# Attention: a head's gate steps and transposes spread over the next head, and the second map's factor as two tensor_tensor steps

## The chip, the cores and the metric

The kernel runs on one NeuronCore of a Trainium2 chip. The metric is the device time of one execution in microseconds (us). TensorE (PE in the profile) multiplies and transposes, VectorE (DVE) and ScalarE (ACT) do elementwise work, GpSimd (POOL) too, and SyncE (SP) issues the DMAs.

## What is computed

One streaming step of a layer with two token mixers: a gated linear recurrence and a differential attention, projected, merged and added to the input. There are 2048 prompt tokens and 64 sample tokens with 4096 cached keys, 8 heads with two maps of 64 channels each, and values of 128 channels. The change lies in the attention and its output norm and gate:

```python
def diff_attn(q, k, v, q_pos, k_pos, rel_bias, lam):
    s = jnp.einsum('bqhmd,bkhmd->bhmqk', q, k) * (DK ** -0.5)
    s = jnp.where(visible, s + bias, -jnp.inf)
    p = jax.nn.softmax(s, axis=-1)
    w = p[:, :, 0] - lam * p[:, :, 1]
    return jnp.einsum('bhqk,bkhd->bqhd', w, v)

o = rms_norm(o, subln_gain) * (1.0 - lam_init)
yb = o.reshape(B, T, W_B) * jax.nn.silu(zb)
```

## The kernel before

The program goes through a first stage (norm of the input, recurrence), projections, the attention stage (1659 to 2551 us of the profile), and output projections. Within attention the 8 heads follow each other. A head has 16 query blocks of 128 tokens, taken in 8 pairs in the order `ORDER`, large beside small, and a block of sample queries (`sample_score_units`, `sample_turn_units`) between them.

A query block's scores come, for each of the two maps, in units of up to 1024 columns: `product` (L942, L943) writes them into a bank `pk` (two buffers), `evacuate` empties it on VectorE with the bias added and the maximum taken (L955, L963) into `S0`/`S1` or, for short blocks, `T0`/`T1`. L972 makes the maximum `nm`; ScalarE takes the exponential with its sum (L973). Behind the second map, VectorE computes the factor `cf` = -lambda · sum0 / sum1, one element a partition: a reciprocal (L978) and a step with two products (L979). GpSimd multiplies the second map by `cf` (L980) and adds it to the first (L981). Then TensorE transposes the result in groups of up to four (L1000), ScalarE copies it (L1001), and TensorE multiplies it with the values (L1008). The sample's scores come in four steps of 1024 cached keys (L1063) and one of 64 new ones (L1077); VectorE evicts the first two into `SA` and the next two into `SB` (L1067, the last in two pieces, L1072), and the fifth by L1078.

When a head's last value product is done, `finish` runs in the time of the next head: it computes the norm's factor with small steps (L1155 to L1160 and three rounds of `newton`, L55 to L57), and then for five chunks of up to four query blocks `weigh` loads the gate `zt` (three buffers) and does one `scalar_tensor_tensor` (L1172) for each block, 17 for a head; `part` transposes them (L1182) into `ptt` (three buffers), evicts that with a gain into `yt` (L1184, two buffers) and stores it in `yb_d` (L1185).

TensorE's order in this stage is written by a planner: a loop with a model time `pe[0]` takes score, transpose and value units as they come due. `extras` holds work with a due time; its entries run as soon as `pe[0]` has reached it. `finish` is such an entry, `part` of chunk j another, due 12 + 1.5·j model-us later (3 + 1.5·j in the last head); `weigh` runs in `finish` itself, for all five chunks. The order on VectorE, ScalarE, GpSimd and SyncE is chosen by the scheduler from this program.

Of the kernel before, what the change touches and what calls it, by code (L numbers as in the profile page):

```python
# [14 lines left out]
ALU = mybir.AluOpType  # L15
# [10 lines left out]
NH = 8  # L26
# [301 lines left out]
def stream_step_kernel(ctx, tc, I, O):  # L328
    nc = tc.nc
# [27 lines left out]
    neglam = cst.tile([P, 1], F32, name="neglam")  # L357
# [505 lines left out]
    with ExitStack() as c:  # L863
# [57 lines left out]
        def score_units(h, hd, Q, i, st):  # L921
# [23 lines left out]
            def evacuate(m, u):  # L945
# [8 lines left out]
                if f > 0:  # L954
                    nc.vector.tensor_scalar(  # L955
                        s[:, k0 : k0 + f], pk[:, :f], far[:, h : h + 1], None,
                        op0=ALU.add, op1=ALU.max, accum_out=mp[:, cx["j"] : cx["j"] + 1],
                    )
                    cx["j"] += 1
                if f < w:  # L960
# [4 lines left out]
                        op0=ALU.add, op1=ALU.max, accum_out=mp[:, cx["j"] : cx["j"] + 1],  # L965
# [4 lines left out]
                sc = [st[f"s{r}"][:, i : i + 1] for r in range(2)]  # L970
# [5 lines left out]
                S = cx["S"]  # L976
                cf = wk.tile([P, 1], F32, name="cf", bufs=4)
                nc.vector.reciprocal(cf, sc[1])  # L978
                nc.vector.scalar_tensor_tensor(cf, cf, sc[0], neglam, op0=ALU.mult, op1=ALU.mult)  # L979
                nc.gpsimd.tensor_scalar(S[1][:, :n], S[1][:, :n], cf, 1.0, op0=ALU.mult, op1=ALU.mult)  # L980
                nc.gpsimd.tensor_tensor(S[0][:, :n], S[0][:, :n], S[1][:, :n], op=ALU.add)  # L981

# [168 lines left out]
        def finish(h, t0, n, st):  # L1151
# [12 lines left out]
            def weigh(b, nb):  # L1164
                tn = TOK[b][1]
                zt = wk.tile([P, 4, P], F32, name="zt", bufs=3)
                nc.sync.dma_start(
                    zt[:tn, :nb, :], zb_d[b : b + nb, :tn, h * P : (h + 1) * P].rearrange("b p c -> p b c")
                )
                for j in range(nb):  # L1170
                    k = b + j
                    nc.vector.scalar_tensor_tensor(  # L1172
                        o[:tn, k, :], o[:tn, k, :], y[:tn, k - t0 : k - t0 + 1], zt[:tn, j, :],
                        op0=ALU.mult, op1=ALU.mult,
                    )
                book("dve", pe[0] + 2.0, 0.25 * nb)
# [10 lines left out]
            for j, b in enumerate(range(t0, t0 + n, 4)):  # L1187
                nb = min(4, t0 + n - b) if b < NT - 1 else 1
                if b < NT - 1 < b + nb:
                    nb = NT - 1 - b  # L1190
                weigh(b, nb)
                extras.append([pe[0] + (12.0 if h < NH - 1 else 3.0) + 1.5 * j, 0.11 * nb,
                               lambda b=b, nb=nb: part(b, nb)])


# [1 line left out]
        pe = [0.0]  # L1197
# [25 lines left out]
        extras = []  # L1223
# [329 lines left out]
```

## Time and profile before

| | |
|---|---|
| time, median of 3 (lowest, highest) | 3129.71 us (3129.59, 3131.15) |
| the profiled execution: time, span | 3132.76 us, 3131.0 us |
| mean granted clock of TensorE | 0.958 |
| busy in the whole span: PE, DVE, ACT, POOL | 91%, 66%, 54%, 46% |
| L979, 128 times | 65.1 us of DVE |
| L1172, 128x128, 128 times | 48.4 us of DVE |
| L1184, 128x512, 31 times | 23.1 us of DVE |

A row of the timeline is one instruction, or several of one kind in a row ("x12", with the length of all). In brackets stands the idle time of the engine before it, and what ended that. An instruction that is held while it executes is shown longer, not as idle. In the table by stretch, the granted clock stands as a share of 2.4 GHz; the lower level, 1.2 GHz, is 0.5.

### The profile page before, as it was taken

To read this page: it belongs to the slowest core of one execution; us is meant where nothing else is said; L and a number is where in the kernel's file an instruction comes from. 1 tells how busy PE (TensorE), PEld (TensorE's weight loads), DVE (VectorE), ACT (ScalarE), POOL (GpSimd) and SP (SyncE) were. 2 spreads that over 40 slices of the span, in tenths; PEclk is the share of its full clock that TensorE was granted. 3 is DMA by queue.
4 is the path that set the end of the run, shared out by engine and by line. 5 is a ranking of instruction groups with operands and counts; after the bars stand their busy time and mean duration, and the time that the engine had idled before them with its cause. 6 is when DMAs were issued, how large, how long until landed. Compare 5 with 4: busy or idle time off the path is not lost.

```text
span 3131.0 us, 43652 instructions
## 1 busy us (share of the span) xinstructions
PE 2854.5 (91%) x14808; PEld 2392.7 (76%) x14808; DVE 2070.2 (66%) x4147; ACT 1703.7 (54%) x3251; POOL 1447.7 (46%) x900
## 2 busy tenths in 40 slices
PE   6999996999979989699997998998999979979899
PEld 6888885777758777587785987887888768868677
DVE  7776786267685776735525677777777775475764
ACT  7776774345544455545445766676676653333432
POOL 0000005355454544545544655555465457786743
PEclk9999998999989999899998999999999989989999
DMA  4121232335534346354346453544543434545553
GB/s 139 60 75 53 70 122 84 124 128 149 181 100 156 129 131 184 108 165 138 107 117 170 124 141 112 144 127 122 135 117 116 128 101 148 196 149 196 177 172 129
DMA packets 356671, 408.96 MB, mean 131 GB/s; under 512 B 48448, under 2 KB 242400, under 8 KB 356448
## 3 DMA queue, kind: packets, MB, share of 16 engines
q1 hardware_dynamic: 356448, 406.18, 42.3%
q8 instruction: 117, 1.92, 0.3%
q14 instruction: 106, 0.87, 0.1%
HBM read 272.22 MB, written 131.37 MB: 129 GB/s over the span
## 4 chain that ended last, share of the span: by engine, by line
PE 45%; DVE 11%; ACT 4%; issue 2%; POOL 2%; DMA 1%; SPq 0%; DVEq 0%; POOLq 0%; ACTq 0%
PE acc L65 7%; PE acc L63 7%; PE acc L64 7%; PE accv L1008 5%; PE pk L942 3%; PE pk L943 3%; PE ptt L1000 3%; PE accv L1131 2%; PE acz L65 1%; PE acz L63 1%; PE acz L64 1%; DVE o L1172 1%; DVE S L955 1%; ACT S L973 1%; DVE w L135 1%
## 5 line engine op out<-in xcount | busy, mean ns | idle before, releaser
L65 PE MATMUL acc<-w,x 128*128 128x512 f32 x1728 | 694.9, 402 | 82.8 <-POOL x L181 55.4
L63 PE MATMUL acc<-w,x 128*128 128x512 f32 x1728 | 699.0, 405 | 14.8 <-ACT sc L230 7.7
L64 PE MATMUL acc<-w,x 128*128 128x512 f32 x1728 | 689.0, 399 | 11.2 <-DVE w L145 10.8
L65 PEld LDWEIGHTS acc<-w,x 128*128 128x128 f32 x1728 | 334.8, 194 | 168.6 <-POOL x L181 64.1
L145 POOL TENSOR_TENSOR w<-w,w 128x1024 fp32r<-128x1024 f32 x63 | 180.1, 2860 | 574.7 <-ACT w L143 549.4
L63 PEld LDWEIGHTS acc<-w,x 128*128 128x128 f32 x1728 | 335.7, 194 | 87.1 <-ACT sc L230 8.5
L64 PEld LDWEIGHTS acc<-w,x 128*128 128x128 f32 x1728 | 335.2, 194 | 81.8 <-DVE w L145 11.8
L181 POOL TENSOR_TENSOR x<-xA,x 128x512 fp32r<-128x512 f32 x144 | 217.3, 1509 | 311.9 <-ACT x L178 298.2
L942 PE MATMUL pk<-k,Q 128*128 128x512 f32 (+2 forms) x640 | 263.2, 413 | 48.8 <-DVE S L955 17.7
L955 DVE TENSOR_SCALAR_CACHE_REDUCE S<-pk,far 128x1024 f32<-128x1024 f32 x224 | 226.2, 1014 | 118.5 <-PE pk L943 105.3
L1008 PE MATMUL accv<-v,tw 128*128 128x128 f32 x2176 | 295.7, 279 | 2.6 <-ACT o L1020 2.3
L1008 PEld LDWEIGHTS accv<-v,tw 128*128 128x128 f32 x2176 | 271.8, 195 | 9.2 <-ACT o L1020 4.2
L1001 ACT COPY tw<-ptt 128x512 f32<-128x512 f32 (+1 forms) x288 | 157.5, 556 | 150.3 <-PE ptt L1000 148.6
L973 ACT ACTIVATE S<-S,nm 128x1920 f32<-128x1920 f32 (+7 forms) x128 | 208.7, 1631 | 52.7 <-DVE nm L972 52.4
L64 PE MATMUL accb<-x,wh 128*128 128x384 f32 (+3 forms) x656 | 232.9, 355 | 2.9 <-DVE x L515 2.9
L181 POOL TENSOR_TENSOR x<-xS,x 128x512 fp32r<-128x512 f32 x144 | 209.9, 1462 | 54.0 <-ACT x L178 52.1
L63 PE MATMUL accb<-x,wh 128*128 128x384 f32 (+3 forms) x656 | 234.4, 357 | 0.2 <-ACT x L514 0.2
L981 POOL TENSOR_TENSOR S<-S,S 128x2048 f32<-128x2048 f32 (+3 forms) x64 | 232.5, 3633 | 4.4
L65 PE MATMUL accb<-x,wl 128*128 128x384 f32 (+3 forms) x656 | 232.8, 355 | 0.0
L943 PE MATMUL pk<-k,Q 128*128 128x512 f32 (+2 forms) x640 | 231.6, 368 | 0.0
L181 DVE TENSOR_TENSOR x<-xA,x 128x512 fp32r<-128x512 f32 x144 | 145.8, 1012 | 122.9 <-ACT x L178 122.9
L178 ACT CAST x<-xA 128x512 fp32r<-128x512 f32 x288 | 177.3, 621 | 75.0 <-PE acc L65 38.2
(253 smaller groups left out, 6152.9 us busy)
## 6 DMA issues: line engine op xcount, KB each, us to landing
xA<-xn_d SPq DMA_DIRECT2D x192, 256.0 KB, 3.0
w<-in_wg SPq DMA_DIRECT2D x72, 512.0 KB, 5.7
raw<-in_ckT SPq DMA_DIRECT2D x32, 512.0 KB, 4.2
Q<-qh_d SPq DMA_DIRECT2D x128, 128.0 KB, 2.8
Q<-ql_d SPq DMA_DIRECT2D x128, 128.0 KB, 2.9
raw<-in_cv SPq DMA_DIRECT2D x32, 512.0 KB, 3.9
raw<-in_w1b SPq DMA_DIRECT2D x32, 256.0 KB, 3.1
ya_d<-SZ SPq DMA_DIRECT2D x16, 512.0 KB, 3.3
```

The source lines that it names most:

```text
L63: nc.tensor.matmul(out, shi, mhi, start=start, stop=False, **kw)
L64: nc.tensor.matmul(out, shi, mlo, start=False, stop=False, **kw)
L65: nc.tensor.matmul(out, slo, mhi, start=False, stop=stop, **kw)
L145: eng.tensor_tensor(lo[:, s, :], raw[:, s, :], hi.bitcast(F32)[:, s, :], op=ALU.subtract)
L178: nc.scalar.copy(xs[nm][0], q[nm])
L181: eng.tensor_tensor(xs[nm][1], q[nm], xs[nm][0].bitcast(F32), op=ALU.subtract)
L942: nc.tensor.matmul(pk[:, o], Q[0][:, m, qs], kk, start=True, stop=False)
L943: nc.tensor.matmul(pk[:, o], Q[1][:, m, qs], kk, start=False, stop=True)
L955: nc.vector.tensor_scalar(s[:, k0 : k0 + f], pk[:, :f], far[:, h : h + 1], None, op0=ALU.add, op1=ALU.max, accum_out=mp[:, cx["j"] : cx["j ...
L973: nc.scalar.activation(s[:, :n], s[:, :n], AF.Exp, bias=nm, accum_out=sc[m])
L981: nc.gpsimd.tensor_tensor(S[0][:, :n], S[0][:, :n], S[1][:, :n], op=ALU.add)
L1008: nc.tensor.matmul(acc[:, r, :], tw[:, j, :], hd[kt // 8][1][:, kt % 8, :], start=kt == r == 0, stop=kt == 2 * p + 1)
```

## The change

`weigh` of chunk j becomes an entry of `extras` of its own, due 4·j model-us after `finish`, and `part` of chunk j is due 12 + 4·j after it. For the last head all stays as it was. The step with two products becomes two `tensor_tensor` steps: `cf` times sum0, then times -lambda. Lines behind L979 count one more in the changed kernel.

```diff
--- before.py
+++ after.py
@@ -976,7 +976,8 @@
                 S = cx["S"]
                 cf = wk.tile([P, 1], F32, name="cf", bufs=4)
                 nc.vector.reciprocal(cf, sc[1])
-                nc.vector.scalar_tensor_tensor(cf, cf, sc[0], neglam, op0=ALU.mult, op1=ALU.mult)
+                nc.vector.tensor_tensor(cf, cf, sc[0], op=ALU.mult)
+                nc.vector.tensor_tensor(cf, cf, neglam, op=ALU.mult)
                 nc.gpsimd.tensor_scalar(S[1][:, :n], S[1][:, :n], cf, 1.0, op0=ALU.mult, op1=ALU.mult)
                 nc.gpsimd.tensor_tensor(S[0][:, :n], S[0][:, :n], S[1][:, :n], op=ALU.add)
 
@@ -1188,8 +1189,11 @@
                 nb = min(4, t0 + n - b) if b < NT - 1 else 1
                 if b < NT - 1 < b + nb:
                     nb = NT - 1 - b
-                weigh(b, nb)
-                extras.append([pe[0] + (12.0 if h < NH - 1 else 3.0) + 1.5 * j, 0.11 * nb,
+                if h == NH - 1:
+                    weigh(b, nb)
+                else:
+                    extras.append([pe[0] + 4.0 * j, 0.0, lambda b=b, nb=nb: weigh(b, nb)])
+                extras.append([pe[0] + (12.0 + 4.0 * j if h < NH - 1 else 3.0 + 1.5 * j), 0.11 * nb,
                                lambda b=b, nb=nb: part(b, nb)])
```

The instructions outside the attention stage keep their order. VectorE has 128 instructions more; the other engines have the same ones in another order. (A number behind a name tells apart the tiles of one name.)

VectorE at the finish of head 0, in the time of head 1, in the kernel before (`SA` and `SB` are the sample's evictions, `o` the gate steps):

```order
L57 SCALAR_TENSOR_TENSOR yo<-e_15360,yo 128x17
L1172 SCALAR_TENSOR_TENSOR o<-o,yo,zt 128x128 x12
L1067 TENSOR_SCALAR SA,mps<-pk,far 128x1024
L1067 TENSOR_SCALAR SB,mps<-pk,far 128x1024
L1172 SCALAR_TENSOR_TENSOR o<-o,yo,zt 128x128 x4
L1172 SCALAR_TENSOR_TENSOR o<-o,yo,zt 64x128
L1067 TENSOR_SCALAR SB,mps<-pk,far 128x896
```

VectorE at the finish of head 0 in the changed kernel:

```order
L57 SCALAR_TENSOR_TENSOR yo<-e_15382,yo 128x17
L1173 SCALAR_TENSOR_TENSOR o<-o,yo,zt 128x128 x5
L1068 TENSOR_SCALAR SA,mps<-pk,far 128x1024
L1173 SCALAR_TENSOR_TENSOR o<-o,yo,zt 128x128 x7
L1068 TENSOR_SCALAR SB,mps<-pk,far 128x1024
L1173 SCALAR_TENSOR_TENSOR o<-o,yo,zt 128x128 x4
L1173 SCALAR_TENSOR_TENSOR o<-o,yo,zt 64x128
L1068 TENSOR_SCALAR SB,mps<-pk,far 128x896
```

The twelve gate steps ahead of the second `SA` eviction are now five and seven, with the eviction between them; the row ends as before.

VectorE at the finish of head 1 in the kernel before:

```order
L1172 SCALAR_TENSOR_TENSOR o<-o,yo,zt 128x128 x12
L978 RECIPROCAL cf<-s_16183 128x1
L1067 TENSOR_SCALAR SA,mps<-pk,far 128x1024
L1172 SCALAR_TENSOR_TENSOR o<-o,yo,zt 128x128 x4
L979 SCALAR_TENSOR_TENSOR cf<-cf,s_16182,neglam 128x1
L1172 SCALAR_TENSOR_TENSOR o<-o,yo,zt 64x128
L1067 TENSOR_SCALAR SA,mps<-pk,far 128x1024
L1184 TENSOR_SCALAR yt<-ptt,gs 128x512
L1067 TENSOR_SCALAR SB,mps<-pk,far 128x1024
L1184 TENSOR_SCALAR yt<-ptt,gs 128x512 x2
L1067 TENSOR_SCALAR SB,mps<-pk,far 128x896
```

VectorE at the finish of head 1 in the changed kernel:

```order
L1173 SCALAR_TENSOR_TENSOR o<-o,yo,zt 128x128 x4
L978 RECIPROCAL cf<-s_16215 128x1
L1068 TENSOR_SCALAR SA,mps<-pk,far 128x1024
L979 TENSOR_TENSOR cf<-cf,s_16214 128x1
L1173 SCALAR_TENSOR_TENSOR o<-o,yo,zt 128x128
L980 TENSOR_TENSOR cf<-cf,neglam 128x1
L1173 SCALAR_TENSOR_TENSOR o<-o,yo,zt 128x128 x9
L1068 TENSOR_SCALAR SA,mps<-pk,far 128x1024
L1173 SCALAR_TENSOR_TENSOR o<-o,yo,zt 128x128 x2
L1173 SCALAR_TENSOR_TENSOR o<-o,yo,zt 64x128
L1068 TENSOR_SCALAR SB,mps<-pk,far 128x1024
```

The factor's steps stood behind 16 gate steps and now stand behind 4 and 5; the second `SA` eviction stood behind 16 and the short one and now stands behind 14, and two `yt` evictions are gone from between the sample's.

VectorE at the start of head 2, the second and the third factor, in the kernel before:

```order
L978 RECIPROCAL cf<-s_16183 128x1
L979 SCALAR_TENSOR_TENSOR cf<-cf,s_16182,neglam 128x1
L955 TENSOR_SCALAR S_16471,mp<-pk,far 128x1024
L955 TENSOR_SCALAR S_16471,mp<-pk,far 128x512
L978 RECIPROCAL cf<-s_16183 128x1
L963 ISA S_16471,mp<-pk,band 128x256
L963 ISA mp 128x1
L979 SCALAR_TENSOR_TENSOR cf<-cf,s_16182,neglam 128x1
L972 TENSOR_REDUCE nm<-mp 128x1
L955 TENSOR_SCALAR S_16494,mp<-pk,far 128x1024
L955 TENSOR_SCALAR S_16494,mp<-pk,far 128x512
```

VectorE at the start of head 2 in the changed kernel, where each factor takes two steps:

```order
L978 RECIPROCAL cf<-s_16215 128x1
L979 TENSOR_TENSOR cf<-cf,s_16214 128x1
L955 TENSOR_SCALAR S_16507,mp<-pk,far 128x1024
L980 TENSOR_TENSOR cf<-cf,neglam 128x1
L955 TENSOR_SCALAR S_16507,mp<-pk,far 128x512
L978 RECIPROCAL cf<-s_16215 128x1
L963 ISA S_16507,mp<-pk,band 128x256
L963 ISA mp 128x1
L979 TENSOR_TENSOR cf<-cf,s_16214 128x1
L955 TENSOR_SCALAR S_16530,mp<-pk,far 128x1024
L980 TENSOR_TENSOR cf<-cf,neglam 128x1
L972 TENSOR_REDUCE nm<-mp 128x1
```

Between the two halves of a factor stands an eviction of 1024 columns now, and the 512-column one stands behind the second half. At the starts of heads 1, 3, 5 and 7 the third factor's halves have such an eviction between them, too.

GpSimd at the start of head 2 in the kernel before (L980 multiplies, L981 adds):

```order
L980 TENSOR_SCALAR S_16336<-S_16336,cf 128x1920
L980 TENSOR_SCALAR T_16405<-T_16405,cf 128x256
L981 TENSOR_TENSOR S_16292<-S_16292,S_16336 128x1920
L981 TENSOR_TENSOR T_16400<-T_16400,T_16405 128x256
L980 TENSOR_SCALAR T_16442<-T_16442,cf 128x128
```

GpSimd at the start of head 2 in the changed kernel:

```order
L981 TENSOR_SCALAR S_16369<-S_16369,cf 128x1920
L982 TENSOR_TENSOR S_16325<-S_16325,S_16369 128x1920
L981 TENSOR_SCALAR T_16439<-T_16439,cf 128x256
L982 TENSOR_TENSOR T_16434<-T_16434,T_16439 128x256
L981 TENSOR_SCALAR T_16477<-T_16477,cf 128x128
```

The step of 1920 columns that adds the maps now stands ahead of the multiplication of the 256-column block.

## Rows read from the trace of the kernel before

**Rows 1.** The table by stretch, the attention stage: busy us of PE to POOL, granted clock, DMA
```profile
1659.00:2551.00 892.00, 823.74 (x5621) 717.84 (x5621) 652.76 (x2100) 593.26 (x1253) 483.33 (x292) 0.97 0.45 125
```

**Rows 2.** The waits of PE in the attention stage: total us, times, longest
```profile
PE pk L942 <- DVE S L955: 17.7, 21, 2.0
PE pk L1063 <- DVE SA L1067: 17.1, 4, 4.3
```

**Rows 3.** Groups by line, VectorE, the line of the factor: busy us, mean ns
```profile
L979 DVE SCALAR_TENSOR_TENSOR cf<-cf,s,neglam 128x1 f32<-128x1 f32 x128 | 65.1, 508 | 1.5
```

**Rows 4.** The timeline of VectorE and GpSimd, first stage: start, us, instruction
```profile
742.67 1.09 DVE L55 SCALAR_TENSOR_TENSOR tmpa<-ya 128x16 f32<-128x16 f32 x1
743.79 1.20 DVE L56 TENSOR_TENSOR tmpa<-tmpa,va 128x16 f32<-128x16 f32 x1
...
742.44 1.29 POOL L181 TENSOR_TENSOR x<-xS,x 128x512 fp32r<-128x512 f32 x1
743.69 1.28 POOL L173 TENSOR_TENSOR xA<-xA,xA 128x512 f32<-128x512 f32 x1
```

**Rows 5.** The timeline of VectorE, GpSimd and TensorE, start of head 2
```profile
1890.45 1.73 DVE L979 SCALAR_TENSOR_TENSOR cf<-cf,s,neglam 128x1 f32<-128x1 f32 x1
...
1894.38 2.71 DVE L979 SCALAR_TENSOR_TENSOR cf<-cf,s,neglam 128x1 f32<-128x1 f32 x1
...
1892.79 4.29 POOL L981 TENSOR_TENSOR S<-S,S 128x1920 f32<-128x1920 f32 x1
...
1891.01 1.16 PE L1008 MATMUL accv<-v,tw 128*128 128x128 f32 x8
1893.44 0.50 PE L942 MATMUL pk<-k,Q 128*128 128x512 f32 x1 [1.27 <-DVE S L955]
...
1898.41 0.50 PE L942 MATMUL pk<-k,Q 128*128 128x512 f32 x1 [0.63 <-DVE S L955]
```

**Rows 6.** The timeline of VectorE and GpSimd, start of head 1
```profile
1781.36 0.22 DVE L979 SCALAR_TENSOR_TENSOR cf<-cf,s,neglam 128x1 f32<-128x1 f32 x1
...
1781.90 4.31 POOL L981 TENSOR_TENSOR S<-S,S 128x1920 f32<-128x1920 f32 x1
```

**Rows 7.** The timeline of VectorE, GpSimd and TensorE, finish of head 0
```profile
1802.92 6.66 DVE L1172 SCALAR_TENSOR_TENSOR o<-o,yo,zt 128x128 f32<-128x128 f32 x12
...
1802.83 3.72 POOL L981 TENSOR_TENSOR S<-S,S 128x1664 f32<-128x1664 f32 x1
...
1810.84 2.85 PE L1063 MATMUL pk<-raw,Qs 128*128 128x512 f32 x4 [4.29 <-DVE SA L1067]
```

**Rows 8.** The table by stretch, behind an even finish and near 2480
```profile
1811.50:1815.00 3.50, 3.50 (x12) 2.12 (x11) 3.07 (x10) 0.36 (x1) 0.00 (x0) 0.55 0.62 219
...
2480.00:2488.00 8.00, 6.60 (x29) 5.73 (x28) 5.02 (x22) 4.99 (x14) 3.42 (x4) 0.57 0.63 183
```

**Rows 9.** The timeline of VectorE and TensorE, finish of head 6
```profile
2478.12 0.75 DVE L1184 TENSOR_SCALAR yt<-ptt,gs 128x512 f32<-128x512 f32 x1 [2.44 <-DMA yb_d<-yt]
...
2478.93 0.28 PE L1182 MATMUL ptt<-ident,o 64*128 64x64 f32 x1 [1.99 <-DVE nm L972]
```

**Rows 10.** The timeline of VectorE, GpSimd and TensorE, finish of head 1
```profile
1910.48 3.24 DVE L1172 SCALAR_TENSOR_TENSOR o<-o,yo,zt 128x128 f32<-128x128 f32 x12
...
1915.96 0.21 DVE L979 SCALAR_TENSOR_TENSOR cf<-cf,s,neglam 128x1 f32<-128x1 f32 x1
...
1918.06 1.27 DVE L1067 TENSOR_SCALAR_CACHE_REDUCE SA<-pk,far 128x1024 f32<-128x1024 f32 x1
...
1923.18 0.75 DVE L1184 TENSOR_SCALAR yt<-ptt,gs 128x512 f32<-128x512 f32 x1 [1.32 <-DMA yb_d<-yt]
...
1916.34 1.66 POOL L980 TENSOR_SCALAR S<-S,cf 128x1664 f32<-128x1664 f32 x1 [5.95 <-DVE cf L979]
1918.08 3.71 POOL L981 TENSOR_TENSOR S<-S,S 128x1664 f32<-128x1664 f32 x1
...
1925.31 0.47 PE L942 MATMUL pk<-k,Q 128*128 128x512 f32 x1 [1.85 <-issue]
```

## The prediction

> **What bounds the kernel now.** I read the busy shares by stretch first. In the attention stage (1659 to 2551 us) TensorE is busy for 823.74 of 892.00 us [rows 1], VectorE for 652.76, GpSimd for 483.33. So TensorE sets the end, and what can be won or lost by moving other engines' work is its idle time of some 68 us and the stretches where its granted clock falls. The view of waits says where that idle time lies: 17.7 us before a score product that waits until VectorE has emptied a bank of scores (L955), and 17.1 us, four times 4.3, before a sample-score product that waits for VectorE's `SA` eviction (L1067) [rows 2]. Both are waits for VectorE's place in a row of work, not for its total. Then I read the timelines at the places where a head begins and where the norm of the head before (`finish`) falls into it. These repeat with two heads, so that heads 2, 4 and 6 look alike, and heads 1, 3, 5 and 7. The change touches nothing outside this stage.
>
> **The factor as two steps, by itself.** It adds 128 VectorE instructions of one element a partition. A free-running `cf` step takes about 0.22 us [rows 6], and the 128 have a mean of 508 ns [rows 3]: 128 × (0.508 - 0.22) = 37 us of that line is waiting. The stalled ones start while a GpSimd step L980 or L981 is in flight and end when it ends: the one at 1890.45 lasts 1.73, and the one at 1894.38 lasts 2.71 and ends at 1897.09, as the L981 step at 1892.79 (4.29 us) does at 1897.08 [rows 5]. Is a `tensor_tensor` held in the same way? No tensor_tensor of the attention stage meets GpSimd, but one in the first stage does: at 743.79 a 128x16 step of L56 takes 1.20 us and ends with the GpSimd step that began at 743.69 (1.28 us); the step before it, 742.67 to 743.76, ends with the GpSimd step before that one [rows 4]. So it is held as well, and GpSimd's next step gets in between two held VectorE steps. The Trainium skill ("SBUF — State Buffer", section "Who interferes with whom") says the same against this part of the change: a VectorE instruction with two SBUF inputs and a GpSimd instruction that reads SBUF shut each other out for a whole instruction; by it the split saves none of the 37 us, and without it the sum would be that of the third rival.
>
> Two steps for one therefore cost about 0.15 us more where nothing holds them (128 × 0.15 = 19 us of VectorE, which has 892 - 653 = 239 us free, so nothing on TensorE), and give two chances of being held instead of one. What matters is what now stands between the two steps. The order of the changed kernel shows it.
>
> **Start of heads 2, 4 and 6.** Before, the second factor is held 1.73 us at 1890.45, the third 2.71 us at 1894.38, and TensorE waits 1.27 at 1893.44 and 0.63 at 1898.41 for the evictions behind them [rows 5]. After, a 1024-column eviction stands between the two halves of the second factor, and GpSimd's L981 step of 1920 columns (4.29 us) now stands ahead of the short step that needs this factor. It starts by 1892.6, so the second half, ready about 1893.75 behind the eviction, is held to about 1896.9, and the 512-column eviction behind it ends at about 1897.8 instead of about 1894. The third factor is then hardly held, which gives back most: its following 1024-column eviction ends at about 1899.6 instead of 1898.3. TensorE waits for that bank. I take +1.2 us (bounds 0, if its later waits take it up, and +2.5): 3 × 1.2 = +3.6.
>
> **Start of heads 1, 3, 5 and 7.** Before, the third factor takes 0.22 us at 1781.36, just ahead of the 4.31 us step at 1781.90 [rows 6], and TensorE doesn't stop. After, a 1024-column eviction (1.27) stands between its halves, so the second half is ready at about 1783 and held until about 1786.4, and the 512-column eviction behind it comes 3.4 us late. TensorE has two score banks, and about 1.5 us of other products to do until it needs that one: it waits up to 2. Bounds 0 and +2.2; I take +1.0, as part of it falls out of the wait at the finish that follows: 4 × 1.0 = +4.0.
>
> **Even finishes (heads 0, 2, 4).** Before, 12 gate steps L1172 run from 1802.92 for 6.66 us; the first is held behind the GpSimd step 1802.83 (3.72 us). The `SA` eviction follows, and TensorE idles 4.29 us to 1810.84 [rows 7]. The clock that it is granted in the 3.5 us after is 0.55, that is the 1.2 GHz level for most of it [rows 8]. After, 5 steps precede the eviction, not 12. The first step is held till 1806.55 and the other 11 take 3.0 us; 7 steps fewer are 1.9 us. That is the gain that the chunks can give here. Against it: all 17 gate steps still stand ahead of the last `SB` eviction, so that VectorE's row ends when it did; and the sample product stands earlier in TensorE's order, with two groups of three transposes and four products moved from before it to after it (eight products take 1.16 us at 1891.01 [rows 5]; with the transposes about 2.0 for the two groups), so TensorE arrives earlier and idles 4.3 + 2.0 - 1.9 = 4.4 us, after which the clock falls as now. Work only moved past a wait costs nothing, so I take +0.5 (bounds -1.9 and +0.9): 3 × 0.5 = +1.5.
>
> **Finish of head 6.** Here four transposes' results wait for buffers: VectorE stands still 2.44 us at 2478.12 for the store of `yt` (two buffers), TensorE 1.99 us behind it [rows 9], and the granted clock between 2480 and 2488 is 0.57 [rows 8]. With `part` spaced 4 model-us instead of 1.5, the stores are done in time. That returns 1.99 + about 1.65 (half of 3.3 us spent at the low level): -3.6 (bounds -5 and 0).
>
> **Odd finishes (heads 1, 3, 5).** Before, the 12 gate steps run freely from 1910.48 (3.24 us), because GpSimd has nothing to do: its next factor is ready only at 1915.96, behind 16 gate steps, and its L981 step (3.71 us) lies at 1918.08 beside evictions from PSUM, which aren't held. The `SA` eviction starts at 1918.06, the third `yt` waits 1.32 us for a store at 1923.18, and TensorE stops 1.85 at 1925.31 [rows 10]. After, the factor's halves come after 4 and 5 gate steps. So GpSimd's pair of 1.66 and 3.71 us starts with 9 to 10 gate steps to go, and by the alternation of [rows 4] holds one step for about 1.6 and one for 3.7: +5.3 us ahead of the second `SA` eviction, less 3 gate steps that moved behind it (0.8): +4.5. Behind it, two of the three `yt` evictions (0.75 each) and the 1.32 us wait are gone from VectorE's row: -2.8. The last `SB` eviction is thus about 1.7 later. I take +1.5 for TensorE (bounds -4, if the waits for stores were what counted, and +5, if its wait for `SA` is long enough to lower the clock): 3 × 1.5 = +4.5.
>
> **Sum.** 3.6 + 4.0 + 1.5 - 3.6 + 4.5 = +10.0 us. The profiled execution took 3132.76 us, so it would be 3142.8; the median of before, 3129.71, is 3.05 lower: 3139.7, say 3140. SP's order changes with the `zt` loads; each still has three buffers and is asked for ahead of its chunk, and I cost that at nothing: the loads are hidden by the gate steps of the chunk before, and if that cover goes, it is about 1.3 us a finish.
>
> **The rivals.** A measurement of this kernel can tell about 0.2% (6.3 us) from no change.
> *First, the delays are taken up.* Each start's delay falls out of the waits for `SA` (17.1 us in all [rows 2]) that follow. Then the two starts cost nothing, and 1.5 - 3.6 + 4.5 = +2.4 is left: 3132. For it: these waits exist at every even finish. Against: none follows at odd ones. 0.22.
> *Second, the spreading works as such.* The sample evictions get through earlier by 1.9 at four finishes (-7.6), the stops at the end of odd finishes go (about 3 × 1.9 = -5.6), -3.6 at head 6, and the starts cost half (+3.8): -13.0, 3117. For it: TensorE's waits are for places in VectorE's row, which the change alters. Against: 17 gate steps still lie within one finish in VectorE's order. 0.18.
> *Third, a `tensor_tensor` of one element isn't held*, or hardly. Then the waits of the starts go (1.27 + 0.63 and some more, say 2.6 × 3 = -7.9, instead of +7.6), and 1.5 - 3.6 + 4.5 stays: -5.5, 3124. [Rows 4] speak against it. 0.08.
> *Fourth, worse than forecast:* the wait for `SA` at odd finishes becomes 5 to 6 us and lowers the clock as at even ones [rows 8], +5 each instead of +1.5, and starts at their upper bounds: 7.5 + 8.8 + 1.5 - 3.6 + 15 = +29; with half of the excess, +20: 3150. [...] 0.10.
>
> **How the numbers follow.** The forecast (+10, 3140) has 0.42. Slower by over 0.2%: 0.42 + 0.10 = 0.52; within: 0.22; faster: the second and about all of the third, 0.26. The range leaves out the far half of the second and the upper part of the fourth: 3120 to 3154. The predicted time is the forecast's.
>
> **What would show it.** Right: the two lines of the factor in the changed profile have over 37 us of waiting between them; at the starts of heads 2, 4 and 6 a second half of about 3 us; GpSimd's 1664-column steps within the gate steps of odd finishes, with single gate steps of 1.6 and 3.7 us; no wait of `yt` for stores. Wrong: second halves of 0.2 us beside GpSimd steps in flight (third rival); TensorE's waits for `SA` under 3 us (second rival); waits at starts that reappear as shorter waits at finishes (first rival).

## The result, and the profile of the changed kernel

The changed kernel takes 3160.33 us (median; 3159.52 the lowest) where the kernel before takes 3129.71: a ratio of 1.0095, 95% interval 1.0066 to 1.0124. It is slower, which was the likeliest case, but by 30.6 us, not by 10; the range ended at 3154. One of its three executions took 3636.15 us at a mean granted clock of 0.742 and is left out of the ratio. The profiled execution has a span of 3157.7 us, 26.8 more than before.

Waits of TensorE in the attention stage, changed kernel (total us, times, longest); before, [rows 2], the first two were 17.7 behind L955 and 17.1 for `SA`:

```profile
PE pk L942 <- DVE mp L963: 24.9, 17, 3.5
PE pk L1064 <- DVE SA L1068: 20.4, 6, 4.9
PE pk L942 <- DVE S L955: 13.3, 16, 1.6
PE ptt L1001 <- ACT tw L1002: 12.2, 3, 4.1
```

The wait for the maximum piece `mp` of an eviction is 24.9 us now, it was 12.2; that for ScalarE's copies (L1002) is 12.2, it was 3.6. The copies' 12.2 us are three waits of 4.1, one at each odd finish.

Groups by line, VectorE (busy us, mean ns); L979 was 65.1 us in one step, [rows 3]:

```profile
L979 DVE TENSOR_TENSOR cf<-cf,s 128x1 f32<-128x1 f32 x128 | 65.4, 511 | 1.4
L980 DVE TENSOR_TENSOR cf<-cf,neglam 128x1 f32<-128x1 f32 x128 | 37.7, 295 | 1.9
...
L1173 DVE SCALAR_TENSOR_TENSOR o<-o,yo,zt 128x128 f32<-128x128 f32 x128 | 63.7, 560 | 0.3
...
L1185 DVE TENSOR_SCALAR yt<-ptt,gs 128x512 f32<-128x512 f32 x31 | 23.1, 746 | 7.1 <-PE ptt L1183 5.1 <-DMA yb_d<-yt 1.4 <-PE pk L943 0.6
```

The first half of the factor alone costs what the whole did, the second half 37.7 us more. Of these 103 us some 41 are work (128 × 2 × 0.16, the length of a half that nothing holds); the other 62 are waiting. The gate steps were 48.4 us and are 63.7: 15 us of new waiting. The wait of `yt` for stores fell from 8.4 to 1.4 us, and that of the gate steps for their `zt` loads from 2.7 to nothing, so these loads were rightly put at nothing.

To see where the 26.8 us arise I put the two profiled executions side by side at the same landmarks: the reciprocal (L978) of the first and of the fifth factor of each head, and the end. The stretch from first to fifth is the start of a head; the stretch from the fifth to the next head's first holds the finish of the head before. The growth of the delay, in us:

| stretch | forecast | measured | one by one |
|---|---|---|---|
| start of head 0 and its rest | 0 | -4.0 | |
| starts of heads 1, 3, 5, 7 | +4.0 | +13.2 | 2.5, 1.8, 4.4, 4.6 |
| starts of heads 2, 4, 6 | +3.6 | +5.8 | 1.9, 1.9, 2.0 |
| even finishes (heads 0, 2, 4; 6 with the end) | -2.1 | +1.4 | 2.1, 0.7, 1.0, -2.5 |
| odd finishes (heads 1, 3, 5) | +4.5 | +11.4 | 3.6, 4.6, 3.1 |
| ahead of attention | 0 | -1.1 | |
| sum | +10.0 | +26.8 | |

The stretch ahead of attention differs by -4 to +1 us between runs of kernels that are alike there, so a sum of a profile is good to a few us only.

The start of head 2 in the changed kernel, VectorE, GpSimd, TensorE (before: [rows 5]):

```profile
1889.96 1.77 DVE L979 TENSOR_TENSOR cf<-cf,s 128x1 f32<-128x1 f32 x1
1891.65 1.27 DVE L955 TENSOR_SCALAR_CACHE_REDUCE S<-pk,far 128x1024 f32<-128x1024 f32 x1
1892.86 3.24 DVE L980 TENSOR_TENSOR cf<-cf,neglam 128x1 f32<-128x1 f32 x1
1896.02 0.74 DVE L955 TENSOR_SCALAR_CACHE_REDUCE S<-pk,far 128x512 f32<-128x512 f32 x1
...
1891.81 4.27 POOL L982 TENSOR_TENSOR S<-S,S 128x1920 f32<-128x1920 f32 x1
...
1892.99 0.50 PE L942 MATMUL pk<-k,Q 128*128 128x512 f32 x1 [1.31 <-DVE S L955]
1897.22 0.50 PE L942 MATMUL pk<-k,Q 128*128 128x512 f32 x1 [1.26 <-DVE mp L963]
```

(Counted within its head this is the third factor, and that of the next rows the fourth; the prediction counted one too few.) Its second half is held 3.24 us until GpSimd's step at 1891.81 ends at 1896.08, and the eviction of 512 columns behind it waits for it. TensorE's two stops, 1.31 and 1.26, are the evictions on either side of it. This hold was forecast nearly to the tenth (1893.75 to 1896.9, that is 3.15 us).

The start of head 1 (before: [rows 6], no stop):

```profile
1777.96 3.52 DVE L980 TENSOR_TENSOR cf<-cf,neglam 128x1 f32<-128x1 f32 x1
1781.41 0.74 DVE L955 TENSOR_SCALAR_CACHE_REDUCE S<-pk,far 128x512 f32<-128x512 f32 x1
...
1782.56 0.50 PE L942 MATMUL pk<-k,Q 128*128 128x512 f32 x1 [1.49 <-DVE mp L963]
1783.99 0.50 PE L942 MATMUL pk<-k,Q 128*128 128x512 f32 x1 [0.46 <-DVE S L955]
```

The factor's second half is held 3.52 us, and TensorE stops 1.49 and 0.46. Heads 3, 5 and 7 are not like head 1 in the changed kernel, though the section on the change and the prediction took them to be: there the eviction of 1024 columns stands ahead of both halves of the fourth factor, and it is the first half that is held. The start of head 5, VectorE, GpSimd and TensorE, and the stretch behind the stop:

```profile
2233.22 3.73 DVE L979 TENSOR_TENSOR cf<-cf,s 128x1 f32<-128x1 f32 x1
...
2232.65 4.28 POOL L982 TENSOR_TENSOR S<-S,S 128x1920 f32<-128x1920 f32 x1
...
2238.70 0.80 PE L942 MATMUL pk<-k,Q 128*128 128x512 f32 x1 [3.46 <-DVE mp L963]
...
2238.70:2246.10 7.40, 7.40 (x34) 6.78 (x35) 4.40 (x11) 3.80 (x5) 0.01 (x1) 0.62 0.00 1
```

TensorE stops once, for 3.46 us, and for 3.47 at heads 3 and 7. Behind it the granted clock (the third figure from the right) is 0.62, mostly the 1.2 GHz level; at head 7 it is 0.61, but at head 3 it stays at 1.00. Why it falls at two of the three, no run shows.

The finish of head 1, in the time of head 2 (before: [rows 10]):

```profile
1905.00 0.15 DVE L980 TENSOR_TENSOR cf<-cf,neglam 128x1 f32<-128x1 f32 x1
...
1907.36 3.80 DVE L1161 TENSOR_SCALAR yo<-yo 128x17 int32<-128x17 int32 x1
1911.08 0.14 DVE L972 TENSOR_REDUCE nm<-mp 128x1 f32<-128x3 f32 x1
...
1915.84 7.29 DVE L1173 SCALAR_TENSOR_TENSOR o<-o,yo,zt 128x128 f32<-128x128 f32 x9
1923.06 1.27 DVE L1068 TENSOR_SCALAR_CACHE_REDUCE SA<-pk,far 128x1024 f32<-128x1024 f32 x1
...
1905.33 1.76 POOL L981 TENSOR_SCALAR S<-S,cf 128x1792 f32<-128x1792 f32 x1 [5.40 <-DVE q L1157]
1907.17 3.96 POOL L982 TENSOR_TENSOR S<-S,S 128x1792 f32<-128x1792 f32 x1
...
1916.10 1.79 POOL L981 TENSOR_SCALAR S<-S,cf 128x1664 f32<-128x1664 f32 x1 [3.01 <-DVE cf L980]
1917.97 3.70 POOL L982 TENSOR_TENSOR S<-S,S 128x1664 f32<-128x1664 f32 x1
...
1903.48 1.05 ACT L1002 COPY tw<-ptt 128x512 f32<-128x512 f32 x2
...
1911.32 1.68 ACT L973 ACTIVATE S<-S,nm 128x1664 f32<-128x1664 f32 x1 [4.29 <-DVE nm L972]
...
1913.00 1.54 ACT L1002 COPY tw<-ptt 128x512 f32<-128x512 f32 x3
...
1913.62 1.11 PE L1001 MATMUL ptt<-ident,S 128*128 128x128 f32 x4 [4.08 <-ACT tw L1002]
1924.39 1.98 PE L1064 MATMUL pk<-raw,Qs 128*128 128x512 f32 x4 [1.34 <-DVE SA L1068]
```

Nine gate steps take 7.29 us: two were held by GpSimd's pair, 1.66 and 3.88 us. But TensorE's long stop isn't there. It ends at 1913.62, 4.08 us long, and the way back is: ScalarE's copies at 1913.00, behind the exponential at 1911.32, which waited 4.29 us for the maximum at 1911.08, which stood in VectorE's row behind a small step of the norm, held 3.80 us by GpSimd's step at 1907.17, whose pair began only at 1905.33, since the second half of the fifth factor (1905.00) stands behind an eviction.

The same chain stands in the kernel before, with a norm step held 3.62 us, but there TensorE stops 0.81 us for it (ScalarE and TensorE, before):

```profile
1903.89 1.54 ACT L1001 COPY tw<-ptt 128x512 f32<-128x512 f32 x3
...
1911.24 0.66 PE L1000 MATMUL ptt<-ident,S 128*128 128x128 f32 x4 [0.81 <-ACT tw L1001]
```

Counted from the reciprocal of the fifth factor (1903.32; before, 1901.87), the waiting exponential starts 8.0 us later now, and 7.1 before. But TensorE runs out of work 6.2 us behind that reciprocal now, and 8.6 before. The maximum next before the one waited for stood ahead of the factor (1902.02), and now stands behind its second half (1905.07). Its exponential is later by that, and on ScalarE only two copies (1903.48), not three (1903.89), get through ahead of the exponential that waits.

The granted clock behind the stop of 4.08 us, in the table by stretch (the last three figures are clock, DMA share, GB/s):

```profile
1913.60:1917.00 3.40, 3.38 (x14) 3.07 (x15) 3.40 (x12) 1.53 (x3) 0.90 (x1) 0.55 0.26 80
```

0.55: mostly the 1.2 GHz level. The even finish of head 0, VectorE and TensorE (before: [rows 7]):

```profile
1800.37 4.80 DVE L1173 SCALAR_TENSOR_TENSOR o<-o,yo,zt 128x128 f32<-128x128 f32 x5
1805.10 1.27 DVE L1068 TENSOR_SCALAR_CACHE_REDUCE SA<-pk,far 128x1024 f32<-128x1024 f32 x1
...
1806.43 3.78 PE L1064 MATMUL pk<-raw,Qs 128*128 128x512 f32 x4 [4.93 <-DVE SA L1068]
```

Five gate steps, the first held, instead of twelve; yet TensorE stops 4.93 us instead of 4.29, as it arrives earlier.

### The profile page after: what moved, and what is told of

Its sections match the earlier page's. It is cut to its first block, busy times and chain, and to the rows that moved or that the text cites. A ratio compares the mean times of both kernels' runs of the same rounds, so it can differ in the third digit from the quotient of the medians.

```text
span 3157.7 us, 43820 instructions
## 1 busy us (share of the span) xinstructions
PE 2863.1 (91%) x14808; PEld 2396.3 (76%) x14808; DVE 2112.9 (67%) x4275; ACT 1706.0 (54%) x3251; POOL 1445.9 (46%) x900
## 4 chain that ended last, share of the span: by engine, by line
PE 43%; DVE 12%; ACT 4%; issue 2%; POOL 2%; DMA 1%; SPq 0%; POOLq 0%; DVEq 0%; ACTq 0%
PE acc L65 7%; PE acc L63 7%; PE acc L64 7%; PE accv L1009 5%; PE pk L942 3%; PE pk L943 3%; PE ptt L1001 2%; PE accv L1132 2%; DVE o L1173 2%; DVE S L955 1%; PE acz L65 1%; PE acz L63 1%; PE acz L64 1%; ACT S L973 1%; DVE cf L979 1%
## 5 line engine op out<-in xcount | busy, mean ns | idle before, releaser
L955 DVE TENSOR_SCALAR_CACHE_REDUCE S<-pk,far 128x1024 f32<-128x1024 f32 x224 | 226.4, 1015 | 126.2 <-PE pk L943 108.4
L942 PE MATMUL pk<-k,Q 128*128 128x512 f32 (+2 forms) x640 | 265.8, 416 | 48.7 <-DVE mp L963 24.9
L1002 ACT COPY tw<-ptt 128x512 f32<-128x512 f32 (+1 forms) x288 | 157.9, 555 | 177.2 <-PE ptt L1001 176.3
L981 POOL TENSOR_SCALAR S<-S,cf 128x2048 f32<-128x2048 f32 (+3 forms) x64 | 103.9, 1624 | 253.8 <-DVE cf L980 140.0
```

The costliest lines, as they stand in the source:

```text
L942: nc.tensor.matmul(pk[:, o], Q[0][:, m, qs], kk, start=True, stop=False)
L955: nc.vector.tensor_scalar(s[:, k0 : k0 + f], pk[:, :f], far[:, h : h + 1], None, op0=ALU.add, op1=ALU.max, accum_out=mp[:, cx["j"] : cx["j ...
L1002: nc.scalar.copy(tw[:, : len(srcs), :], ptt[:, : len(srcs), :])
```

## The experiments

Theory A at first: held halves of the factor make the loss at the starts, and the collision of gate steps with GpSimd's pair that at odd finishes. The rivals were that the chunks' new places in TensorE's order make it (B, D), or the mere place of two steps and not the hold (G). Two runs, e8 and e12, leave the product with `zt` out of the computation. The table has every run: the median, its ratio to the kernel before, run beside it, with the 95% interval, and, from the profiled executions, the growth of the delay by stretch as above.

| run | us | ratio (interval) | odd starts | even starts | even finishes | odd finishes |
|---|---|---|---|---|---|---|
| changed kernel | 3160.33 | 1.0095 (1.0066 to 1.0124) | +13.2 | +5.8 | +1.4 | +11.4 |
| e1, two steps only | 3169.66 | 1.0129 (1.0113 to 1.0145) | +12.9 | +5.8 | 0.0 | +21.1 |
| e2, chunks only | 3148.69 | 1.0060 (1.0045 to 1.0075) | +3.7 | -0.9 | -1.5 | +15.7 |
| e3, factor with one tensor input | 3120.38 | 0.9969 (0.9959 to 0.9979) | 0.0 | -7.4 | -2.8 | +3.1 |
| e4, factor on GpSimd | 3135.12 | 1.0016 (1.0006 to 1.0026) | 0.0 | -7.6 | -3.1 | +17.3 |
| e5, chunks and e3's factor | 3124.49 | 0.9979 (0.9969 to 0.9990) | -5.4 | -7.5 | -1.7 | +12.6 |
| e6, gate steps later only | 3142.71 | 1.0045 (1.0030 to 1.0060) | +3.7 | -0.9 | -7.4 | +15.5 |
| e7, transposes later only | 3148.45 | 1.0062 (1.0042 to 1.0082) | +5.7 | +10.1 | -11.4 | +14.0 |
| e8, changed, gate steps not held, no product with `zt` | 3144.36 | 1.0048 (1.0033 to 1.0064) | +9.4 | +5.8 | -6.7 | +7.4 |
| e9, two steps, one tensor input each | 3123.27 | 0.9972 (0.9962 to 0.9982) | 0.0 | -7.6 | -0.2 | +2.4 |
| e10, changed kernel with e9's factor | 3124.71 | 0.9981 (0.9971 to 0.9990) | -5.4 | -7.7 | -4.7 | +16.1 |
| e11, e3 with the gate on GpSimd | 3115.64 | 0.9951 (0.9936 to 0.9965) | +0.2 | -7.3 | -4.0 | -0.9 |
| e12, e10 with e8's gate steps, no product with `zt` | 3099.31 | 0.9899 (0.9883 to 0.9916) | -5.3 | -7.5 | -13.3 | -3.7 |
| e13, e5 with e11's gate | 3106.97 | 0.9921 (0.9904 to 0.9939) | -5.3 | -7.3 | -4.2 | -4.2 |

**e1: only the factor in two steps.**

```diff
-nc.vector.scalar_tensor_tensor(cf, cf, sc[0], neglam, op0=ALU.mult, op1=ALU.mult)
+nc.vector.tensor_tensor(cf, cf, sc[0], op=ALU.mult)
+nc.vector.tensor_tensor(cf, cf, neglam, op=ALU.mult)
```

> The kernel before with only the factor's part of the change: two tensor_tensor steps; the gate steps and transposes stay as before. TensorE's order is then that of before, word for word. Theory A (the factor's halves, with evictions between them, are held behind GpSimd and make the stops at the starts of heads): the steps at the starts of heads (heads 1, 3, 5, 7: +2.5, +1.8, +4.4, +4.6; heads 2, 4, 6: +1.9 each; later in odd heads +0.85 each, head 0: -5.1) belong to it, sum +17: about 3147 us. Theory B (those steps are TensorE work that the chunks moved there, and the split alone costs what was forecast, +7.6, less head 0's 5.1): about 3132 us.

3169.66, that is 39.6 us slower than before beside it: more than the whole change (though the two intervals just overlap), and more than either theory said. The starts sum up to those of the changed kernel (+12.9, +5.8; at heads 3, 5 and 7 with stops like head 1's, 1.49 and 0.46), so B falls: TensorE's order is that of before here. What A had not seen is +21 at the odd finishes, without any chunks. VectorE and TensorE there:

```profile
1917.47 6.25 DVE L1173 SCALAR_TENSOR_TENSOR o<-o,yo,zt 128x128 f32<-128x128 f32 x5
1931.26 0.75 DVE L1185 TENSOR_SCALAR yt<-ptt,gs 128x512 f32<-128x512 f32 x1 [3.81 <-DMA yb_d<-yt]
...
1933.39 0.56 PE L942 MATMUL pk<-k,Q 128*128 128x512 f32 x1 [4.67 <-issue]
```

The five gate steps behind the factor are held, the third `yt` waits 3.81 us for a store, and TensorE stops 4.67 us, besides the 4.09 at ScalarE's copies that the changed kernel has too. So in the changed kernel the chunks took some 9 us of the split's loss back (9.7 at the odd finishes): their later transposes don't wait for stores.

**e2: only the chunks** (the second part of the diff, the factor in one step).

> The kernel before with only the chunks (weigh due 4j later, part due 12 + 4j later); the factor stays one scalar_tensor_tensor. Theory A: only the odd finishes (+3.7 each) and the even ones (+1.3, -0.1, +0.2, -4.3) are left, +8: about 3138 us. Theory B: about 3129.7 + 30.6 - 2 = 3158 us. Both expect single gate steps of 1.6 and 3.7 us at odd finishes, since the factor stands behind 4 and 5 gate steps there in this order, too.

3148.69, 18.6 slower: between the theories. The split's 39.6 and the chunks' 18.6 don't add up to 30.6. The starts are nearly clean; the loss is at the odd finishes, where the factor stands behind four and five gate steps in this order as well and TensorE stops 4.85 us for `SA`.

**e3: the factor as one step with one tensor input.**

```diff
-nc.vector.scalar_tensor_tensor(cf, cf, sc[0], neglam, op0=ALU.mult, op1=ALU.mult)
+nc.vector.tensor_scalar(cf, cf, sc[0], neglam, op0=ALU.mult, op1=ALU.mult)
```

> The kernel before with the factor as one tensor_scalar with both multipliers as scalar operands, so that it reads one tensor from SBUF and not two. TensorE's and GpSimd's orders are those of before. Theory A1 (the step is held because it reads two tensors from SBUF): line L979 falls from 65 to about 28 us (128 x 0.22), the stops of 1.27, 0.63 and 0.72 at the starts of heads 2, 4, 6 and those at head 0's start go: 8 to 13 us faster, about 3119 us. Theory A2 (any step between tiles of SBUF is held, as L1160, a tensor_scalar, is for 3.62 us): L979 stays near 65 us and the time near 3130.

3120.38, 9.7 faster, and the row of L979 (min/median/max ns) says A1:

```profile
L979 DVE TENSOR_SCALAR cf<-cf,s,neglam x128: 264/272/277, 1672.2 to 2522.6; 128x1 f32<-128x1 f32 x128
```

No one of 128 is held, beside the same GpSimd steps that held it up to 3628 ns. The Trainium skill ("SBUF — State Buffer", section "Who interferes with whom") counts `tensor_scalar` among the steps that can be held when they run in a mode with two ports, and one with at most one SBUF input outside these modes among those that can't. The trace agrees as far as it goes: the step of one element is never held, while the one of 128x17 (L1160) still is, for up to 3.63 us; which mode either ran in, no row shows. TensorE's, GpSimd's and ScalarE's orders are those of before and VectorE's differs in 2 of 3507 steps, so the 9.7 us are the hold's.

**e4: the factor on GpSimd** (`nc.gpsimd.tensor_scalar` in its place).

> The kernel before with the factor's step on GpSimd itself (tensor_scalar with two scalar operands), so that VectorE never waits for it. VectorE loses 65 us of line L979, GpSimd gets 128 steps of perhaps 0.1 to 0.4 us. If the holds of the factor cost TensorE what theory A says, 8 to 13 us faster, about 3119 us; if GpSimd's row is what sets the end at the starts of heads, no gain, 3130 us.

3135.12, 5 slower. The starts gain just as in e3; all is lost at the odd finishes (+17.3). The group of the line on GpSimd:

```profile
L979 POOL TENSOR_SCALAR cf<-cf,s,neglam 128x1 f32<-128x1 f32 x128 | 43.8, 343 | 278.0 <-DVE cf L978 188.7 <-DVE nm L972 52.0 <-ACT tw L1001 23.6
```

Without a wait on VectorE the factor and GpSimd's pair come sooner, among the gate steps, one of which is held 3.89 us; TensorE then stops 1.79 and 4.15 us. An early factor is no gain where the pair that follows it holds others.

**e5: chunks with e3's factor.**

> The changed kernel's chunks with the factor of run e3 (one tensor_scalar that is never held: 264 to 277 ns). Theory A (two causes: held factor steps at the starts, and GpSimd's 1664-column pair that falls among the gate steps at odd finishes): the starts lose 2.5 to 4.6 us each and head 0's start keeps its gain, the collision at the odd finishes stays, so about e2's 18.6 less e3's 9.7: 3139 us. Theory C (the collision at the odd finishes follows only from late, held factors): it goes too, and the time is near e3's 3120.

3124.49, 24.2 less than e2, with the same orders but for 6 of VectorE's steps: that is what a factor in one held step costs beside these chunks. Of A the mechanism holds (gate steps still held 3.88 us, odd finishes +12.6), but its sum of 3139 was too high: the chunks also give 1.8 us back at the starts of heads 3, 5 and 7, which only shows when the factor isn't held there.

**e6 and e7: half of the chunks each** (`weigh` due 4j, `part` as before; `part` due 12 + 4j, `weigh` as before).

> The kernel before with the gate steps due 4j later and the transposes as before (12 + 1.5j). Theory A: the gate steps' order is what puts the factor ahead of them at odd finishes, so e2's +18.6 is nearly all here: 3146 us, with single gate steps of 3.9 us at odd finishes; the wait of yt for stores stays (2.4 us at the last even finish). Theory D (the transposes' new places in TensorE's order cost it): about 3130 us.

> The kernel before with the transposes due 12 + 4j and all gate steps in finish itself. Theory A: the stops for stores of yt go (-4.3 at head 6's finish, about -2 at each odd one): 3122 to 3128 us, unless the factor comes ahead of the gate steps here too. Theory D: about 3146 us.

3142.71 and 3148.45: each half alone costs most of the odd finishes (+15.5, +14.0), e7 against A's forecast of a gain. In e7's order, too, the factor of the odd finish stands among gate steps, which are held 1.66 and 3.87 us, and a factor at head 2's start is held 3.70 us. So TensorE's order changes where VectorE's row puts the factor, whichever half is moved. D isn't needed, but these two runs don't rule it out; e12 does.

**e8: the changed kernel with gate steps that aren't held.**

```diff
-nc.vector.scalar_tensor_tensor(o[:tn, k, :], o[:tn, k, :], y[...], zt[:tn, j, :], op0=ALU.mult, op1=ALU.mult)
+nc.vector.tensor_scalar(o[:tn, k, :], o[:tn, k, :], y[...], None, op0=ALU.mult, op1=ALU.max, accum_out=gj[:tn])
```

> The changed kernel with the gate steps as tensor_scalar with an accumulator: one tensor from SBUF instead of two; the product with the gate zt is left out, the number and size of the steps stay. If this form is not held, the 3.6 us at even finishes and the 1.7 and 3.9 us at odd ones go. Theory A: the odd finishes' part of the change goes, 3 x 4 to 5.5, and something at even ones: 3160 - 15 = 3145 us, and the starts' waits stay as in the changed kernel. Theory E (the stop of 4.1 us at the odd finishes, which waits for ScalarE's copies behind a late maximum, and the starts make the loss, not the gate steps): within 5 us of 3160.

3144.36, 16 less than the changed kernel: A's number. But its place is another: nearly half of the gain lies at the even finishes (+1.4 to -6.7), and the odd ones keep +7.4, since the stop of 4.08 us at ScalarE's copies stays. So E has a part, too. At the odd starts 3.8 us go though the stops of 3.4 us stay at heads 3, 5 and 7: the granted clock in the start of head 5 is 1.00 here, and 0.87 in the changed kernel.

**e9: two steps that aren't held, in the same places.**

```diff
-nc.vector.tensor_tensor(cf, cf, sc[0], op=ALU.mult)
-nc.vector.tensor_tensor(cf, cf, neglam, op=ALU.mult)
+nc.vector.tensor_scalar(cf, cf, sc[0], 1.0, op0=ALU.mult, op1=ALU.mult)
+nc.vector.tensor_scalar(cf, cf, neglam, 1.0, op0=ALU.mult, op1=ALU.mult)
```

> Run e1 with both halves of the factor as tensor_scalar steps with one tensor from SBUF each, the form that run e3 showed never to be held. The order keeps the same evictions between the halves at the starts of heads and the same order on GpSimd; only the hold differs. Theory F (the loss of the split is the hold of a second half, 3 us and more, with the eviction behind it): at most 2 to 4 us above e3, 3123 us, no step of the factor over 0.3 us, the stop of 4.1 us for ScalarE's copies at the odd finishes gone or under 2 us. Theory G (it is the place: two steps with evictions between them, and GpSimd's steps later by these): within 10 us of e1, 3160 us or more.

3123.27, the time that F forecast, far from G's. Groups of both halves (busy us, mean ns; 58.2 and 43.6 us in e1):

```profile
L980 DVE TENSOR_SCALAR cf<-cf,neglam 128x1 f32<-128x1 f32 x128 | 27.0, 212 | 1.7
L979 DVE TENSOR_SCALAR cf<-cf,s 128x1 f32<-128x1 f32 x128 | 26.9, 211 | 1.5
```

Between e1 and e9 lie some 46 us (49 by the ratios), and the orders on TensorE and GpSimd and the evictions between the halves are the same. More than the hold differs all the same: the scheduler, given other steps, placed some 60 of VectorE's 3635 steps and 26 of ScalarE's 2809 otherwise. At the starts of heads 1, 3, 5 and 7 only one small maximum has moved, so there the +12.9 of e1, which are 0.0 here, are the hold's. At heads 2, 4 and 6 the maximum beside the fifth factor stands ahead of it again, as in the kernel before, so at the odd finishes (+21.1 against +2.4) hold and order act together, and no run parts them. G is out as far as evictions between the halves and GpSimd's order go. The stop at ScalarE's copies is 1.94 us at the most. Two steps instead of one cost next to nothing by themselves (3123 against e3's 3120).

**e10: the changed kernel with e9's factor.**

> The changed kernel with both halves as in e9. Theory F: near e5 (chunks with a factor that is not held), 3124 to 3128 us; the gate steps of 3.9 us at odd finishes stay. Theory G: within 10 us of 3160 us.

3124.71, 36 less than the changed kernel, with VectorE's and ScalarE's rows placed anew as in e9. What is left is at the odd finishes, VectorE, GpSimd and TensorE:

```profile
1906.43 7.80 DVE L1173 SCALAR_TENSOR_TENSOR o<-o,yo,zt 128x128 f32<-128x128 f32 x11
...
1906.69 1.79 POOL L981 TENSOR_SCALAR S<-S,cf 128x1664 f32<-128x1664 f32 x1 [3.17 <-DVE cf L980]
1908.56 3.70 POOL L982 TENSOR_TENSOR S<-S,S 128x1664 f32<-128x1664 f32 x1
...
1915.50 2.07 PE L1064 MATMUL pk<-raw,Qs 128*128 128x512 f32 x2 [5.41 <-DVE SA L1068]
```

Eleven gate steps take 7.80 us, and TensorE stops 5.41 for `SA`, longer than in the changed kernel: with the first hold gone, it runs into the second.

**e11: towards a faster kernel.** The product with `zt` as one `tensor_tensor` a chunk on GpSimd, the norm's factor in e8's form, on top of e3.

> Towards a faster kernel: e3 with the gate's product taken to GpSimd (one tensor_tensor a chunk of 128x512, five a head) and the norm's factor applied on VectorE by the tensor_scalar with an accumulator that run e8 showed unheld (0.34 us). VectorE's 12 steps ahead of SA then aren't held 3.6 us: the four stops of 4.3 us at even finishes shrink to about 1 and the half clock behind them goes: 3 x 4 + 3 = 10 to 15 us faster than e3, 3108 us. If GpSimd's five steps (about 1.1 us each) come in front of its factor steps, they take that back: 3120 us or more.

3115.64; 5 us under e3, not 12. The stop at head 0's finish is 3.33 us, not 1. All 17 steps stand ahead of the second `SA` eviction there; but in e13, where 7 do, TensorE stops 3.11 us, so their number alone doesn't make it.

**e12: neither the factor nor the gate held.** e10 with e8's gate steps.

> Run e10 with the gate steps in the form of e8 (one tensor from SBUF; the product with the gate zt is left out). At the odd finishes of e10 the gate steps are held 1.65 and 3.87 us by GpSimd's 1664-column pair, and TensorE stops 5.4 us for SA; from the fourth factor of heads 2, 4, 6 to the same place in the next head it loses 5.9, 4.7 and 5.5 us against before. Theory F (the chunks cost by this collision): these three become 2 us or less each, the stop for SA under 2 us, and the even finishes gain some 3 us each as in e8: about 3124.7 - 11 - 10 = 3104 us. Theory H (the chunks cost by TensorE's order, the transposes later, the collision is covered): the three stay at 4 us and more, only the even finishes gain: 3115 us.

3099.31, better than F said. The odd finishes fall from +16.1 to -3.7:

```profile
1908.51 0.34 DVE L1174 TENSOR_SCALAR_CACHE_REDUCE o<-o,yo 128x128 f32<-128x128 f32 x1
...
1908.37 3.70 POOL L982 TENSOR_TENSOR S<-S,S 128x1664 f32<-128x1664 f32 x1
...
1910.37 1.98 PE L1064 MATMUL pk<-raw,Qs 128*128 128x512 f32 x4 [0.34 <-DVE SA L1068]
```

The steps run through GpSimd's 3.70 us unheld, and TensorE waits 0.34 us; H falls, and D with it, as TensorE's order is e10's but for 6 of 14808 steps. The same chunks that cost 18.6 us in e2 are part of the fastest run here.

**e13: the gate on GpSimd, and neither it nor the factor held on VectorE** (e5 with e11's gate; steps of the norm still are, up to 3.63 us).

> The changed kernel's chunks, the factor of e3 (one step, one tensor from SBUF) and the gate of e11 (the product with zt on GpSimd, the norm's factor by the form that isn't held): nothing of the computation is left out. Theory F (e12 gained by steps that are not held): within 5 us of e12's 3099 plus what GpSimd's products cost, 3100 to 3108 us, with a stop for SA at the odd finishes under 2 us. Theory I (e12 gained because zt isn't read, so that no gate step waits for its load): near e11's 3116 or e5's 3124.

3106.97, 0.9921 of before, the fastest kernel with the product in it. The lines that do the gate now, GpSimd and VectorE:

```profile
L1171 POOL TENSOR_TENSOR o<-o,zt 128x512 f32<-128x512 f32 x31 | 40.3, 1301 | 5.9 <-DMA zt<-zb_d 3.1 <-ACT sqo L1023 2.7
...
L1174 DVE TENSOR_SCALAR_CACHE_REDUCE o<-o,yo 128x128 f32<-128x128 f32 x128 | 36.0, 342 | 0.5
```

The product is there again, on GpSimd, and the odd finishes stay at -4.2: the hold of the gate steps was the term, not the waits for `zt`. The 8 us to e12 lie at the even finishes (-4.2 against -13.3).

## Why the prediction was wrong

**The direction, and the mechanism of it, held.** A `tensor_tensor` of one element is held like the step that it replaced; the third rival is out. (That no `tensor_tensor` of the attention stage meets GpSimd was misread: one of L135 at 2526.51 does, and takes 2.42 us where the one before it takes 1.21. It speaks for the hold as well.) The second halves at the starts (3.24 and 3.52 us) and the single gate steps (1.66 and 3.88) are in the trace as forecast, and so, but for 1.4 us, is the end of the waits for stores. First and second rival: the delays were not taken up, and TensorE's waits for `SA` grew from 17.1 to 20.4 us.

**Starts of heads 1, 3, 5, 7: +1.0 each forecast, +3.3 measured in the mean.** Two steps failed. The first is "part of it falls out of the wait at the finish that follows". No part did: the even finishes, which follow these starts, lost 2.1, 0.7 and 1.0 more. In e10, with the same chunks and factors that aren't held, the starts are at -5.4 and the even finishes at -4.7, against +13.2 and +1.4: the held halves cost 18.6 us at the starts (VectorE's rows differ there by one small maximum a head), and nothing comes back behind them. The second is that one row of head 1 stood for all four. "It waits up to 2" is right for head 1 (1.49 and 0.46). At heads 3, 5 and 7, where the scheduler put the eviction ahead of both halves, the wait is 3.47 us, and at heads 5 and 7 the lower clock follows it, some 2.8 us each (an estimate, 0.38 of 7.40 us). Less the 1.8 us that the chunks themselves give there (e5), that is the 1.8, 4.4 and 4.6 measured; the upper bound was 2.2.

**Starts of heads 2, 4, 6: +1.2 forecast, +1.9 measured.** Mechanism and size nearly right; but the base was not zero. Before itself loses 2.5 us at each to its held factor, as e3 shows, and that was to be had.

**Odd finishes: +1.5 each forecast, +3.8 measured in the mean.** The collision was right; the chain was not. I followed only the gate steps to `SA`. I did not follow the fifth factor, whose second half stands behind an eviction too, nor the maximum beside it, which moved behind that second half. So GpSimd's pair comes 1.4 us later, the norm's small step is held till 1911.1, then come the maximum, the exponential, the copies and TensorE; and one copy fewer gets through ahead of that. TensorE stops 4.08 us where it stopped 0.81, and then the clock is lower. The held norm step alone doesn't make it: in e9 the pair is as late and a norm step is held 3.81 us, but with the maximum ahead of the factor TensorE stops 1.94. How much of the rest is the hold at the head's start and how much this order was not tried. Two held rows run beside each other there. Taking one away leaves the other (e8 +7.4, e10 +16.1); taking both gives -3.7 (e12). The fourth rival had the lower clock, and its +29 is near the +26.8 of the profiles; but it set it behind the wait for `SA`, which is 1.34 us at most there. That it came so near is in part luck.

**Even finishes: +0.5 each forecast, some +1.3 measured** (2.1, 0.7, 1.0), and at head 6 -2.5 in place of -3.6, with the end of the kernel in it. The -3.6 contains a slip: a granted clock of 0.57 over 8 us is some 6.9 us at the low level, not 3.3, and half of that is 3.4; so the waits for stores went, and less came of it than the rows allowed.

**Head 0: not costed, -4.0.** Its start has held factors as well; every run without the one held step of before gains 3.9 to 5.0 there, and e2, e6 and e7, which keep it, nothing. In its start TensorE's stops come to some 5.2 us instead of 8.5. Why the split gains here and loses at the other starts was not tried.

In sum the two terms at odd starts and odd finishes are short by 9.2 and 6.9 us, the even starts and finishes by 2.2 and 3.5, and head 0 is 4.0 (with the stretch ahead 5.1) the other way: 16.7, the difference between +10.0 and +26.8.

## What to carry to other kernels

Before an elementwise step is split or moved on an engine that shares something with another, count the tensors that it reads, and look, at every place where it repeats, at what the scheduler puts between and behind the pieces: here 0.15 us of work took 3.2 to 3.7 us where a half met a long step of GpSimd. A form of the step with one tensor input won 9.7 us, moving it to GpSimd lost 5. A delay on the bounding engine is to be counted in full unless a wait is shown that takes it up; and where two rows of held work run beside each other, a test must take away both before it says that neither matters. A test that swaps the form of a step should compare the order of every engine as well, for the scheduler may place the others anew.

## What the runs showed that I had not expected

A `tensor_scalar` of one element a partition is never held beside GpSimd (128 of 128 at 264 to 277 ns, or 211 ns with one constant), and neither is one of 128x128 that also gives an accumulator (342 ns, run e12 beside a 3.70 us step), while the int32 one of 128x17 is (3.80 us). And one change can cost 18.6 us, cost 1 to 4, or win 9, by what stands beside it: the chunks on before, on kernels whose factor isn't held (e5 against e3, e10 against e9), and on e1.
